# The first crossing of a two-block transformer kernel written in source order on three engines

## The chip, the cores and the metric

The kernel runs on one core of a Trainium2 chip. The metric is the device time of one execution in microseconds (us). The engines are named as the profile names them: PE (TensorE, matrix products), PEld (its weight loads), DVE (VectorE), ACT (ScalarE), POOL (GpSimd) and SP (SyncE, which issues the DMAs here). Matrix products and weight loads of PE overlap.

## What is computed

512 tokens of 1024 features pass a first block of two layers and then a second block of one layer. The part that the change touches is the start of a layer of the first block, and the mixers of the second.

```python
def first_block(x, g_pre_mix, w_in, ...):
    cos, sin = rope_tables(s)
    for l in range(DEPTH):                  # DEPTH = 2
        h = rms_norm(x, g_pre_mix[l])
        z = h @ w_in[l]
...
def rms_norm(x, g):
    xf = x.astype(jnp.float32)
    y = xf * lax.rsqrt(jnp.mean(xf * xf, axis=-1, keepdims=True) + RMS_EPS)
    return (y * g.astype(jnp.float32)).astype(x.dtype)
...
def second_block(x, c, rel_bias, ...):
        o_a = diff_attention(..., table_diff, lam_init)
        o_b = forgetting_attention(...)
        o_c = stick_breaking_attention(...)
        o_d = native_sparse_attention(..., table_nsa)
        mixed = jnp.concatenate([o_a, o_b, o_c, o_d], axis=-1) @ w_out[l]
```

Of `z`, the first columns are the queries, then keys and values of a band attention with 16 query heads, 4 key heads of 64 features and a rotary embedding (rope) on queries and keys. `table_diff` gives the differential attention a bias that depends on the distance of two tokens.

## The kernel before

Every fp32 product is made of three products of rounded halves: a tile `x` is split into `hi` (rounded, on ACT) and `lo = x − hi` (on DVE). `mm_kb` issues for one block of 128 features ("kb", 8 of them) hi by hi (L523), weight-hi by lo (L524) and weight-lo by hi (L525).

Weights come as units of 128 x 1024 numbers (512 KB), each holding 128 output columns for all 1024 features. `Stream` loads them in order into three raw buffers (L255, on SP), casts a unit to `wh` on ACT (L267) and subtracts to `wl` on DVE (L268); `cut_to(n)` says how far the casts are to be ahead of their use. A raw buffer is free for a further load once its unit is cast and subtracted.

The crossing (`cross`, L473 on) is the passage from one layer to the next, made in two halves of 256 tokens (`HV`). For one half, `chain1` loads x in four tiles of two feature blocks (`xh`), splits each (`scaled_split`: `hh` on ACT L447, `hl` on DVE L448) and adds its squares to `acc` (`add_sq`: squares on ACT L442, the first of them L437, sums on DVE L443). `Head.run` issues the products of the first three weight units with that half: two units of keys and one of queries, gathered in three PSUM tiles `hd`. `fin1` ends the rms norm of the half: eight one-column products of `acc` with ones (`pc`, L416), DVE L420, a power on POOL (L398), a diagonal `dg` on DVE (L427), one product with ones that spreads it (`pb`, L431), and a copy to `R` on ACT (L512). In layer 0 there is no layer ahead to end, and x comes straight from the input.

After the crossing, `layer` issues the values (`pv`, L559 to L561, 96 products of 256 columns), then the Q blocks one after the other (`ps`, 24 products of 512 columns each with one weight unit). `ropeR` (DVE L565) multiplies the rope tables with `R` of both halves; everything after it needs it: for each head `rope` does two steps on DVE (`t`, L573 and the shuffle L574) and two on POOL (L575, L576), and the result is cast and subtracted: KH on ACT (L587, L588) and KL on DVE (L589, L590) for keys, Q on ACT (L605) and DVE (L606) for queries, V on ACT (L596) and DVE (L597) for values. The number of casts ahead at this place is `CA = (3, 4)` for layers 0 and 1.

The order of the instructions of all engines is found by a scheduler that plays the program through a model of the chip, save where a part stands under `manual_schedule`: there the engines named take the order of the source. An engine executes its own list in order; semaphores make it wait for the others.

In the second block the mixers run as a pipeline of stages (`sb` for the stick-breaking heads, then `diff`, `fox` and `nsa`), each with a list of background pieces that prepare the next (`bg_sb` for the stage `sb`). `load_bias` reads the bias of four heads from a table in memory into four tiles F (L884).

Of the kernel before, what the change touches and what calls it, by code (L numbers as in the profile page):

```python
# [17 lines left out]
NB = 8  # L18
# [11 lines left out]
HV = ((0, 256), (256, 512))  # L30
# [249 lines left out]
class Kern:  # L280
# [181 lines left out]
    def cross(self, tail, chain, head, fin, early=0):  # L462
# [14 lines left out]
        if self.xdst[1][3] is not None:  # L477
            self.xsrc = self.xdst

    def chain1(self, i, pend, h, gname, acc2):  # L480
        nc = self.nc
        t0, t1 = HV[i]
        sl = slice(t0, t1)
        if pend:
            acc, mg, sqs = pend
            pb = self.bcast(self.rstd(acc, HV[i], sqs[i]), 2)
            Rp = self.half("Rp")
            nc.scalar.copy(Rp, pb[:, :256])

        def post():  # L490
            for j in range(4):
                xt = self.xload(i, j)
                if pend:
                    self.residual(xt, mg.t[j][:, :, sl], Rp, xt)
                for a in range(2):
                    kb = 2 * j + a
                    self.scaled_split(h.hi[kb][:, sl], h.lo[kb][:, sl], xt[:, a, :], self.col(gname, kb))
                self.add_sq(acc2[:, :, sl], xt, j == 0, nc.vector)
                if pend:
                    self.xstore(xt, i, j)  # L500

        return post
# [11 lines left out]
    def split(self, hi, lo, src):  # L514
        self.nc.scalar.copy(hi, src)
        self.nc.vector.tensor_sub(lo, src, hi.bitcast(F32))
# [23 lines left out]
    def layer(self, l, tail, pend):  # L540
        nc = self.nc
        h = Pair(self, "h", NB)
        acc2 = self.blk("acc2", [P, 2, T], F32)
        rs = {}
        head = Head(self, h, 3, seq=l == 0)
        self.cross(tail, lambda i: self.chain1(i, pend, h, f"g_pre_mix{l}", acc2), head,
                   lambda i: self.fin1(i, acc2, rs), early=1 if l == 0 else 0)
        rp = self.blk("rope", [P, 2, T], F32)
        nc.sync.dma_start(rp, self.a["rope"].rearrange("p (a t) -> p a t", a=2))
        pk = head.ps[0:2]  # L550
# [2 lines left out]
        for kb in range(NB):  # L553
            w = wv[kb // 4]
            sl = slice((kb % 4) * 256, (kb % 4) * 256 + 256)
# [44 lines left out]
        for m in range(NB):  # L600
            q = rope(head.ps[2] if m == 0 else self.mblock(h))
            for j in range(2):
                hd = 2 * m + j
# [580 lines left out]
    def block2(self, tail, pend):  # L1184
        nc = self.nc
        self.b2_consts()
        h = Pair(self, "h2", NB)
        head = Head(self, h, 4)
        acc2 = self.blk("acc2", [P, 2, T], F32)
# [35 lines left out]
        F = {}  # L1225
# [18 lines left out]
        def halves(x, ng):  # L1244
            v = x.rearrange("p t (a b) -> p t a b", a=ng)
            return [v[:, 0:2], v[:, 2:4]]

        def diff_prep():
            F["a"] = self.load_bias(0)
            box["zs"] = self.blk("zs", [P, 4 * 160], F32R)  # L1250
            box["ys"] = self.blk("ys", [P, 4 * 192], F32R)
            for a in range(2):
                t = self.blk("selraw", [P, 704], F32)
                nc.sync.dma_start(t, self.a["sel"][:, a * 704:(a + 1) * 704])
                for b in range(2):
                    nc.scalar.copy(box["zs"][:, (2 * a + b) * 160:(2 * a + b + 1) * 160], t[:, b * 352:b * 352 + 160])
                    nc.vector.tensor_copy(box["ys"][:, (2 * a + b) * 192:(2 * a + b + 1) * 192],
                                          t[:, b * 352 + 160:(b + 1) * 352])
# [63 lines left out]
        def osplit(m):  # L1322
# [4 lines left out]
        av = self.tm_group(h, 256, 4, self.v_pair(Va, 4), 2)  # L1327
# [6 lines left out]
        dfm = [P1(diff_fm, f) for f in range(4)]  # L1334
        sel = [[P1(diff_sel, f, p) for p in range(2)] for f in range(4)]
        bg_sb = [aq[0], aq[1], ak[0], aq[2], ak[1], diff_prep, dfm[0], ak[2], sel[0][0], av[0], dfm[2], sel[0][1],
                 sel[2][0], av[1], sel[2][1]]
        bg_diff = [g272[0], dfm[1], g272[1], sel[1][0], g272[2], dfm[3], g272[3], sel[1][1], sel[3][0], bq[0], ksw_norm,
                   sel[3][1], bq[1], fox_pre, bk[0], bq[2], bk[1], fox_pre2, bv[0], bk[2], P1(fox_q, 0), bv[1],
                   P1(fox_k, 0), P1(fox_k, 1)]  # L1340
# [45 lines left out]
        h = Pair(self, "h3", NB)  # L1386
        head = Head(self, h, self.NH3)
# [386 lines left out]
```

## Time and profile before

| | us |
|---|---|
| runs | 2470.20, 2470.53, 2471.22 |
| median | 2470.53 |
| the profiled execution | 2470.39 |
| its span | 2468.7 |
| PE busy in the span | 2404.3 (97%) |
| DVE busy | 1347.2 (55%) |
| ACT busy | 995.0 (40%) |
| POOL busy | 393.0 (16%) |

The span is the time from the first to the last instruction in the profile; 1.7 us of the profiled execution lie around it. PE stands for 90% of the chain that ended last. A share of busy time is a mean over stages, so what an edit of one stage can do is read from that stage's rows.

### The profile page before, as it was taken

How to read it: one execution, taken by the hardware profiler on the slowest of the kernel's cores; microseconds unless marked ns; L12 is line 12 of the kernel's file. 1: busy time of each engine (PE TensorE's matmuls, PEld its weight loads, DVE VectorE, ACT ScalarE, POOL GpSimd, SP SyncE). 2: the span in 40 equal slices, each digit the busy share in tenths (PEclk: the TensorE clock that was granted, in tenths of full speed). 3: DMA queues.
4: the chain of work that ended last, by engine and by line, in shares of the span. 5: the costliest groups of instructions: out<-in, count | busy, mean ns of one | idle time of the engine just before them, and what ended most of it. 6: DMA issues, size and time to landing. Idle time of an engine off the chain costs nothing.

```text
span 2468.7 us, 32508 instructions
## 1 busy us (share of the span) xinstructions
PE 2404.3 (97%) x12680; PEld 2069.8 (84%) x12680; DVE 1347.2 (55%) x2352; ACT 995.0 (40%) x1804; POOL 393.0 (16%) x437
## 2 busy tenths in 40 slices
PE   8999999999999999999999999999798899999999
PEld 7888888888888887888888888888788878888888
DVE  7777544366532188775443665321667686644531
ACT  4455423442223244554234422232375575333420
POOL 2423001211110033230012111100021133000000
PEclk9999999999999999999999999999899999999999
DMA  4211523355423232213233553232221204233250
GB/s 145 90 65 61 167 94 103 103 197 198 149 86 121 77 115 81 65 61 124 94 103 103 196 194 139 87 119 77 95 81 52 87 25 145 78 102 103 100 173 27
DMA packets 84995, 264.38 MB, mean 107 GB/s; under 512 B 9151, under 2 KB 17983, under 8 KB 84840
## 3 DMA queue, kind: packets, MB, share of 16 engines
q1 hardware_dynamic: 84840, 262.29, 31.5%
q8 instruction: 100, 1.64, 0.3%
q14 instruction: 55, 0.45, 0.1%
HBM read 249.65 MB, written 15.22 MB: 107 GB/s over the span
## 4 chain that ended last, share of the span: by engine, by line
PE 90%; DVE 5%; ACT 3%; issue 1%; POOL 1%; DMA 0%; SPq 0%; ACTq 0%; POOLq 0%; DVEq 0%
PE ps L523 24%; PE ps L525 24%; PE ps L524 24%; PE hd L524 2%; PE hd L525 2%; PE hd L523 2%; PE o L832 2%; PE pt L807 1%; PE tm L1017 1%; PE tm L1018 1%; PE tm L1019 1%; ACT pp L378 1%; PE s L783 1%; PE s L782 1%; PE s L1136 1%
## 5 line engine op out<-in xcount | busy, mean ns | idle before, releaser
L268 DVE TENSOR_TENSOR wl<-raw,wh 128x1024 fp32r<-128x1024 f32 x382 | 470.7, 1250 | 339.5 <-ACT wh L267 273.8
L267 ACT CAST wh<-raw 128x1024 fp32r<-128x1024 f32 x382 | 389.8, 1049 | 182.5 <-DMA raw<-in_w_dram 96.4
L525 PE MATMUL ps<-hh,wl 128*128 128x512 f32 x752 | 296.6, 394 | 5.5 <-DVE wl L268 5.5
L523 PE MATMUL ps<-hh,wh 128*128 128x512 f32 x752 | 295.6, 393 | 2.9 <-ACT wh L267 2.9
L524 PE MATMUL ps<-hl,wh 128*128 128x512 f32 x752 | 295.3, 393 | 0.0
L524 PE MATMUL ps<-hfl,wh 128*128 128x512 f32 x640 | 249.3, 390 | 0.0
L523 PE MATMUL ps<-hfh,wh 128*128 128x512 f32 x640 | 249.1, 390 | 0.0
L525 PE MATMUL ps<-hfh,wl 128*128 128x512 f32 x640 | 248.9, 389 | 0.0
L525 PEld LDWEIGHTS ps<-hh,wl 128*128 128x128 f32 x752 | 141.7, 188 | 33.8 <-DVE wl L268 6.8
L523 PEld LDWEIGHTS ps<-hh,wh 128*128 128x128 f32 x752 | 141.8, 189 | 30.5 <-ACT wh L267 3.4
L524 PEld LDWEIGHTS ps<-hl,wh 128*128 128x128 f32 x752 | 141.8, 189 | 27.6
L525 PE MATMUL ps<-hidh,wl 128*128 128x512 f32 (+1 forms) x396 | 145.1, 366 | 0.0
L523 PE MATMUL ps<-hidh,wh 128*128 128x512 f32 (+1 forms) x396 | 144.9, 366 | 0.0
L524 PE MATMUL ps<-hidl,wh 128*128 128x512 f32 (+1 forms) x396 | 144.7, 365 | 0.0
L525 PEld LDWEIGHTS ps<-hfh,wl 128*128 128x128 f32 x640 | 120.1, 188 | 25.0
L524 PEld LDWEIGHTS ps<-hfl,wh 128*128 128x128 f32 x640 | 120.2, 188 | 24.6
L523 PEld LDWEIGHTS ps<-hfh,wh 128*128 128x128 f32 x640 | 120.0, 188 | 24.8
L378 ACT ACTIVATE pp<-pp,at_nm 128x256 f32<-128x256 f32 (+1 forms) x208 | 114.4, 553 | 62.6 <-DVE at_nm L789 54.3
L712 POOL TENSOR_TENSOR gs<-gs,R 128x512 f32<-128x512 f32 x44 | 70.0, 1590 | 379.1 <-ACT gs L378 368.1
L524 PE MATMUL ps<-h3l,wh 128*128 128x512 f32 x320 | 124.5, 389 | 0.0
L525 PE MATMUL ps<-h3h,wl 128*128 128x512 f32 x320 | 124.5, 389 | 0.0
L523 PE MATMUL ps<-h3h,wh 128*128 128x512 f32 x320 | 124.3, 389 | 0.0
(462 smaller groups left out, 5208.6 us busy)
## 6 DMA issues: line engine op xcount, KB each, us to landing
raw<-in_w_dram SPq DMA_DIRECT2D x382, 512.0 KB, 3.6
adaraw<-in_ada_dram SPq DMA_DIRECT2D x48, 512.0 KB, 5.7
xd<-xh SPq DMA_DIRECT2D x24, 256.0 KB, 2.1
xh<-xd SPq DMA_DIRECT2D x24, 256.0 KB, 3.4
xh<-in_x_dram SPq DMA_DIRECT2D x16, 256.0 KB, 5.1
bias_d<-row_d SPq DMA_DIRECT2D x8, 320.0 KB, 6.1
xd<-fg SPq DMA_DIRECT2D x8, 256.0 KB, 3.2
F<-bias_d SPq DMA_DIRECT2D x8, 256.0 KB, 5.5
```

What stands on the lines that cost most here:

```text
L267: nc.scalar.copy(hi, raw)
L268: nc.vector.tensor_sub(lo, raw, hi.bitcast(F32))
L378: i = nc.scalar.activation(out, in_, func, **kw)
L523: nc.tensor.matmul(ps[:, t], w[0][:, sl], h.hi[kb][:, t], start=first, stop=False)
L524: nc.tensor.matmul(ps[:, t], w[0][:, sl], h.lo[kb][:, t], start=False, stop=False)
L525: nc.tensor.matmul(ps[:, t], w[1][:, sl], h.hi[kb][:, t], start=False, stop=last)
L712: nc.gpsimd.tensor_mul(g, g, self.R)
L782: nc.tensor.matmul(ps[:, :n], q, KH[g][:, LO[i]:HI[i]], start=True, stop=False)
L783: nc.tensor.matmul(ps[:, :n], q, KL[g][:, LO[i]:HI[i]], start=False, stop=True)
L807: nc.tensor.transpose(bank[:, c0:c0 + P], pslice(h, i)[:, c:c + P], self.ident)
L832: nc.tensor.matmul(ps[:, c0:c1], V[j][:, g * P:(g + 1) * P], t[b][:, a, c0:c1], start=(a == 0 and j == 0), stop=(a == 1 and j == 2))
L1017: nc.tensor.matmul(o, h.hi[kb][:, tsl], w[0][:, sl], start=kb == 0 and i == 0, stop=False)
```

## The change

The crossing of layer 0 gets a function of its own, `cross0`, whose instructions on PE, DVE and ACT stand under `manual_schedule` and so run in source order. Weight unit 1 is cast ahead of the later tiles of x; the squares of a tile come behind splits; PE takes the first four feature blocks of two weight units, then the last four, then the third unit; the second half goes tile by tile; both `fin` calls stand at the end. Layer 1 keeps `cross`. In the second block the loads of the bias for the differential attention leave the piece `diff_prep` and become a piece of their own, later in the list `bg_sb`; the scheduler orders the stage anew from that.

```diff
--- before.py
+++ after.py
@@ -477,6 +477,56 @@
         if self.xdst[1][3] is not None:
             self.xsrc = self.xdst
 
+    def cross0(self, h, head, gname, acc2, fin):
+        E = mybir.EngineType
+        xt = {}
+
+        def split(i, j):
+            sl = slice(*HV[i])
+            xt[j] = self.xload(i, j)
+            for a in range(2):
+                kb = 2 * j + a
+                self.scaled_split(h.hi[kb][:, sl], h.lo[kb][:, sl], xt[j][:, a, :], self.col(gname, kb))
+
+        def square(i, j):
+            self.add_sq(acc2[:, :, slice(*HV[i])], xt.pop(j), j == 0, self.nc.vector)
+
+        def unit():
+            head.w.append(self.st.next(ahead=0))
+            head.ps.append(self.ps("hd"))
+
+        def mm(i, j, kbs):
+            for kb in kbs:
+                self.mm_kb(head.ps[j], head.w[j], h, kb, kb == 0, kb == NB - 1, hv=HV[i])
+
+        with self.tc.manual_schedule(engines={E.PE, E.DVE, E.Activation}):
+            unit()
+            split(0, 0)
+            split(0, 1)
+            mm(0, 0, range(4))
+            unit()
+            mm(0, 1, range(4))
+            square(0, 0)
+            split(0, 2)
+            square(0, 1)
+            split(0, 3)
+            mm(0, 0, range(4, 8))
+            mm(0, 1, range(4, 8))
+            unit()
+            square(0, 2)
+            square(0, 3)
+            mm(0, 2, range(8))
+            for j in range(4):
+                split(1, j)
+                square(1, j)
+                for kb in (2 * j, 2 * j + 1):
+                    for n in range(3):
+                        mm(1, n, [kb])
+                if j in (1, 2):
+                    self.st.cut_to(self.st.used + j)
+            fin(0)
+            fin(1)
+
     def chain1(self, i, pend, h, gname, acc2):
         nc = self.nc
         t0, t1 = HV[i]
@@ -542,9 +592,12 @@
         h = Pair(self, "h", NB)
         acc2 = self.blk("acc2", [P, 2, T], F32)
         rs = {}
-        head = Head(self, h, 3, seq=l == 0)
-        self.cross(tail, lambda i: self.chain1(i, pend, h, f"g_pre_mix{l}", acc2), head,
-                   lambda i: self.fin1(i, acc2, rs), early=1 if l == 0 else 0)
+        head = Head(self, h, 3)
+        fin = lambda i: self.fin1(i, acc2, rs)
+        if l:
+            self.cross(tail, lambda i: self.chain1(i, pend, h, f"g_pre_mix{l}", acc2), head, fin)
+        else:
+            self.cross0(h, head, f"g_pre_mix{l}", acc2, fin)
         rp = self.blk("rope", [P, 2, T], F32)
         nc.sync.dma_start(rp, self.a["rope"].rearrange("p (a t) -> p a t", a=2))
         pk = head.ps[0:2]
@@ -1245,8 +1298,10 @@
             v = x.rearrange("p t (a b) -> p t a b", a=ng)
             return [v[:, 0:2], v[:, 2:4]]
 
+        def diff_bias():
+            F["a"] = self.load_bias(0)
+
         def diff_prep():
-            F["a"] = self.load_bias(0)
             box["zs"] = self.blk("zs", [P, 4 * 160], F32R)
             box["ys"] = self.blk("ys", [P, 4 * 192], F32R)
             for a in range(2):
@@ -1334,7 +1389,7 @@
         dfm = [P1(diff_fm, f) for f in range(4)]
         sel = [[P1(diff_sel, f, p) for p in range(2)] for f in range(4)]
         bg_sb = [aq[0], aq[1], ak[0], aq[2], ak[1], diff_prep, dfm[0], ak[2], sel[0][0], av[0], dfm[2], sel[0][1],
-                 sel[2][0], av[1], sel[2][1]]
+                 sel[2][0], av[1], diff_bias, sel[2][1]]
         bg_diff = [g272[0], dfm[1], g272[1], sel[1][0], g272[2], dfm[3], g272[3], sel[1][1], sel[3][0], bq[0], ksw_norm,
                    sel[3][1], bq[1], fox_pre, bk[0], bq[2], bk[1], fox_pre2, bv[0], bk[2], P1(fox_q, 0), bv[1],
                    P1(fox_k, 0), P1(fox_k, 1)]
```

PE at the start of the first half: `hd_168` and `hd_124` are the first unit's tiles, `hd_155` is the second unit's, `pc_277` belongs to the norm. Before:

```order
L523 MATMUL hd_168<-hh_12_129,wh_8_116 128x256
L524 MATMUL hd_168<-hl_13_130,wh_8_116 128x256
L525 MATMUL hd_168<-hh_12_129,wl_9_117 128x256
L523 MATMUL hd_168<-hh_15_138,wh_8_116 128x256
L416 MATMUL pc_277<-ones,acc_7_115 128x1 x4
L524 MATMUL hd_168<-hl_16_139,wh_8_116 128x256
L525 MATMUL hd_168<-hh_15_138,wl_9_117 128x256
L523 MATMUL hd_168<-hh_15_138,wh_8_116 128x256
L524 MATMUL hd_168<-hl_16_139,wh_8_116 128x256
```

and after, the same places of PE's list:

```order
L573 MATMUL hd_124<-hh_13_131,wh_8_118 128x256
L574 MATMUL hd_124<-hl_14_132,wh_8_118 128x256
L575 MATMUL hd_124<-hh_13_131,wl_9_119 128x256
L573 MATMUL hd_155<-hh_11_125,wh_15_149 128x256
L574 MATMUL hd_155<-hl_12_126,wh_15_149 128x256
L575 MATMUL hd_155<-hh_11_125,wl_16_150 128x256
L573 MATMUL hd_155<-hh_11_125,wh_15_149 128x256
L574 MATMUL hd_155<-hl_12_126,wh_15_149 128x256
L575 MATMUL hd_155<-hh_11_125,wl_16_150 128x256
```

The `pc` group has left this place, and after twelve products the second weight unit (`wh_15`) is needed.

PE at the second `pb` (`pb_302` before, `pb_388` after); `pv` are the values' tiles, `ps` the first Q block. Before:

```order
L525 MATMUL hd_170<-hh_18_147,wl_24_163 128x256
L559 MATMUL pv_403<-wh_45_305,hh_10_122 128x256
L560 MATMUL pv_403<-wl_46_306,hh_10_122 128x256
L561 MATMUL pv_403<-wh_45_305,hl_11_123 128x256
L559 MATMUL pv_403<-wh_45_305,hh_10_122 128x256
L560 MATMUL pv_403<-wl_46_306,hh_10_122 128x256
L561 MATMUL pv_403<-wh_45_305,hl_11_123 128x256
L559 MATMUL pv_404<-wh_45_305,hh_10_122 128x256
L560 MATMUL pv_404<-wl_46_306,hh_10_122 128x256
L561 MATMUL pv_404<-wh_45_305,hl_11_123 128x256
L431 MATMUL pb_302<-dg_300,ones 128x256
L559 MATMUL pv_404<-wh_45_305,hh_10_122 128x256
```

and after:

```order
L612 MATMUL pv_406<-wh_35_330,hh_21_178 128x256
L431 MATMUL pb_388<-dg_386,ones 128x256
L613 MATMUL pv_406<-wl_36_331,hh_21_178 128x256
L614 MATMUL pv_406<-wh_35_330,hl_22_179 128x256
L612 MATMUL pv_407<-wh_35_330,hh_21_178 128x256
L613 MATMUL pv_407<-wl_36_331,hh_21_178 128x256
L614 MATMUL pv_407<-wh_35_330,hl_22_179 128x256
L612 MATMUL pv_407<-wh_35_330,hh_21_178 128x256
L613 MATMUL pv_407<-wl_36_331,hh_21_178 128x256
L614 MATMUL pv_407<-wh_35_330,hl_22_179 128x256
L573 MATMUL ps_567<-hh_11_125,wh_50_394 128x512
L574 MATMUL ps_567<-hl_12_126,wh_50_394 128x512
```

The second `pb` stood behind nine `pv` products; now eight `pv` products are left behind it before the first Q block.

ACT at the copies to `R`, with the weight casts ahead of them. Before:

```order
L267 CAST wh_47_311<-raw_160 128x1024
L267 CAST wh_49_317<-raw_166 128x1024
L512 COPY R<-pb_288 128x256
L267 CAST wh_52_397<-raw_309 128x1024
L267 CAST wh_56_501<-raw_315 128x1024
L512 COPY R<-pb_302 128x256
L587 CAST KH_62_517<-t_60_511 64x512
```

and after:

```order
L267 CAST wh_50_394<-raw_212 128x1024
L267 CAST wh_52_400<-raw_301 128x1024
L267 CAST wh_56_504<-raw_334 128x1024
L562 COPY R<-pb_374 128x256
L562 COPY R<-pb_388 128x256
L640 CAST KH_62_520<-t_60_514 64x512
```

The two copies to `R` (L512 before, L562 after) stood apart, with two casts between them; now they follow each other behind the casts of three units.

## Rows read from the trace of the kernel before

**Rows 1.** Windows: us, busy us of each engine (x instructions), PEclk, DMA share, GB/s
```profile
6.66:12.82 6.16, 5.36 (x22) 4.73 (x22) 6.05 (x15) 6.16 (x13) 0.00 (x0) 1.00 1.04 389
...
17.19:60.00 42.81, 42.81 (x293) 39.92 (x292) 30.54 (x52) 17.47 (x30) 14.21 (x11) 1.00 0.26 88
60.00:70.00 10.00, 7.95 (x34) 5.95 (x33) 9.24 (x11) 4.57 (x6) 6.32 (x4) 1.00 0.21 61
```

**Rows 2.** Timeline of PE, first crossing: start, us, line, operation, [idle before <-releaser]
```profile
10.54 0.41 PE L523 MATMUL hd<-hh,wh 128*128 128x256 f32 x1
11.09 1.86 PE L416 MATMUL pc<-ones,acc 128*128 128x1 f32 x8
...
27.48 0.95 PE L416 MATMUL pc<-ones,acc 128*128 128x1 f32 x8
```

**Rows 3.** Timeline of SP, ACT and DVE, the first weights
```profile
3.73 0.94 SPq L255 DMA_DIRECT2D raw<-in_w_dram  x2
...
5.16 1.04 ACT L267 CAST wh<-raw 128x1024 fp32r<-128x1024 f32 x1 [3.07 <-DMA raw<-in_w_dram]
...
6.23 1.23 DVE L268 TENSOR_TENSOR wl<-raw,wh 128x1024 fp32r<-128x1024 f32 x1 [4.93 <-ACT wh L267]
```

**Rows 4.** Tile view of raw, 3.6 to 12.5 us
```profile
DMA to landing us min/median/max: 6.3/6.7/7.1
```

**Rows 5.** Timeline of PE, second half of layer 0's values
```profile
32.92 0.59 PE L431 MATMUL pb<-dg,ones 128*128 128x256 f32 x2
...
43.78 0.40 PE L523 MATMUL ps<-hh,wh 128*128 128x512 f32 x1
```

**Rows 6.** Timelines of ACT, DVE and PE, layer 0
```profile
33.55 0.37 ACT L512 COPY R<-pb 128x256 f32<-128x256 f32 x1 [4.78 <-PE pb L431]
...
33.96 1.23 DVE L565 TENSOR_TENSOR ropeR<-rope,R 128x1024 f32<-128x1024 f32 x1 [3.59 <-ACT R L512]
...
49.36 0.88 DVE L597 SCALAR_TENSOR_TENSOR V<-pv,rs_r,V 128x256 fp32r<-128x256 f32 x2
...
57.96 1.05 ACT L267 CAST wh<-raw 128x1024 fp32r<-128x1024 f32 x1
...
60.14 2.19 DVE L268 TENSOR_TENSOR wl<-raw,wh 128x1024 fp32r<-128x1024 f32 x1
...
62.38 0.50 PE L525 MATMUL ps<-hh,wl 128*128 128x512 f32 x1 [1.64 <-DVE wl L268]
```

**Rows 7.** Timeline of DVE, the same place of layer 1
```profile
900.27 1.23 DVE L565 TENSOR_TENSOR ropeR<-rope,R 128x1024 f32<-128x1024 f32 x1 [3.32 <-ACT R L512]
...
917.38 0.88 DVE L597 SCALAR_TENSOR_TENSOR V<-pv,rs_r,V 128x256 fp32r<-128x256 f32 x2
...
918.88 1.41 DVE L606 TENSOR_TENSOR Q<-t,Q 64x512 fp32r<-64x512 f32 x2
...
921.89 2.73 DVE L606 TENSOR_TENSOR Q<-t,Q 64x512 fp32r<-64x512 f32 x2
924.64 0.69 DVE L573 TENSOR_TENSOR t<-ps,ropeR 128x512 f32<-128x512 f32 x1
...
926.02 2.37 DVE L606 TENSOR_TENSOR Q<-t,Q 64x512 fp32r<-64x512 f32 x2
928.41 2.18 DVE L268 TENSOR_TENSOR wl<-raw,wh 128x1024 fp32r<-128x1024 f32 x1
```

**Rows 8.** Windows of layer 1, PE alone: us, busy us, PEclk, DMA share, GB/s
```profile
923.50:930.60 7.10, 0.78 (x3) 0.86 0.00 0
930.60:935.40 4.80, 4.75 (x11) 0.50 0.35 111
```

**Rows 9.** Tile view of F, 1790 to 1900 us
```profile
L1137 DVE CUSTOM_DVE_ANT_0 pp<-s,F x16: 284/484/686, 1853.3 to 1888.5; 128x384 f32<-128x384 f32 x4, 128x128 f32<-128x128 f32 x4, 128x256 f32<-128x256 f32 x4, 128x512 f32<-128x512 f32 x4
...
DMA to landing us min/median/max: 3.7/5.9/6.0
```

**Rows 10.** Waits of PE: us in total, times, longest
```profile
PE o L1174 <- ACT sbt L515: 2.6, 3, 1.3
```

## Prediction

> **What bounds the kernel now.** I read the windows view first. TensorE (PE) is the bound almost everywhere: from 17.19 to 60.00 us it is busy for all 42.81 us, and in the first stage, 6.66 to 12.82, for 5.36 of 6.16 [rows 1]. In the ten microseconds after 60 it is idle for 10.00 − 7.95 = 2.05 us [rows 1]. An edit of the first crossing can therefore win only three things: idle time ahead of 17 us, time at the lower clock there, and the 2.05 us. It can lose wherever PE is fed just in time.
>
> The PE timeline of the start comes next [rows 2]. The group of eight short `pc` matmuls takes 1.86 us at 11.09 and 0.95 us at 27.48: the first microseconds run at the lower of the two clock levels (1.2 GHz), although the granted-clock column prints 1.00 there. In before, PE gets through 13 `hd` matmuls (the thirteenth starts at 10.54), takes the `pc` group, and goes on at 12.82, the end of the first window of rows 1.
>
> The third view is the chain that PE waits for after 60 us, followed backwards over three engines [rows 6]. PE waits until 62.38 for `wl` of the fourth Q block (DVE, 60.14, 2.19 us). This needs `wh` (ACT, 57.96), which stands behind the K, V and Q casts of the first heads. Those need `ropeR` (DVE, 33.96), which waits for the copy of R of the second half (ACT, 33.55), and that for the second `pb` on PE at 32.92 [rows 5]. So the place of the second `pb` in PE's order sets when the fourth Q block gets its weights, and the slack is already used up: before waits there.
>
> **The change part by part: the start.** The new order does four contraction blocks of `hd0`, 12 matmuls, and then needs unit 1, whose cast now stands ahead of the later splits. What limits that cast is its transfer: issued at 3.73 [rows 3], landing after at least 6.3 us [rows 4], so at about 10.1. Cast 1.04 and subtract 1.23 [rows 3] put `wl` at 12.4, and PE goes on at 12.45 with 14 `hd` matmuls done (two need `wh` alone) where before went on at 12.82 with 13. That is 0.37 plus one matmul of 0.21 ahead. But before took its `pc` group inside that wait; after takes it later, for about 0.8 us (0.95 less the overlap of its end [rows 2]). Net +0.25 us. The bounds are −1.9 (the higher level comes at 12.5 instead of 17.2: 4.7 us of work would shrink by 0.12/0.21, 2.1 less, and with the +0.25 about −1.9) and +0.5. I take +0.25. The squares moved behind the splits I cost at nothing: the next splits of DVE run beside the ten matmuls of `hd1` that are left at 12.45 (2.1 us at 0.21); if that cover is too thin, it is in the +0.5.
>
> **The second `pb`.** Both `fin` calls now stand at the end of the crossing. In PE's order the second `pb` has eight `pv` matmuls left between it and the first `ps` of the Q blocks, which ran at 43.78 [rows 5]; before it had 87. By rows 5: 43.78 + 0.25 − 8 × 0.12 − 0.24 = 42.8. R follows 0.63 later (32.92 to 33.55), `ropeR` 0.41 after that [rows 5, 6]: 43.9 instead of 33.96, **9.9 us later**. The chain `pc`, `rs_v`, power, `dg` between them is covered by some 30 `pv` matmuls of 0.12, about 3.8 us; it costs nothing on PE.
>
> **From `ropeR` to the fourth Q block.** The 72 matmuls of three Q blocks, plus the eight `pv`, keep PE busy until about 60.4 (43.78 + 72 × 0.227 + 0.25). What DVE has to do from `ropeR` to `wl` stands in layer 1 of before, where `pb` is late already and the order on DVE is nearly the one that layer 0 now gets [rows 7]:
> - `ropeR` 900.27 to the first V at 917.38: 17.1 us, with the same list of operations.
> - V, one `t`, a pair of Q, a shuffle, V: 917.38 to 921.89, 4.5 us.
> - then half a Q pair, `t`, shuffle, the other half: a pair takes 1.33 (918.88, 1.41 with overlap), and `t` with shuffle 1.38 (924.64 to 926.02): 2.7 us.
> - `wl` 2.18.
>
> 43.9 + 17.1 + 4.5 + 2.7 = 68.2, and `wl` ends at 70.4; PE goes on at 70.45 instead of 62.38 [rows 6], +8.07. The second wait of before, 2.05 − 1.64 = 0.41 [rows 1, 6], disappears behind it. **+7.7 us.** The +0.25 of the start is inside this sum, not beside it. Bounds: layer 0 of before needed 15.4 us to V (49.36 [rows 6]) plus 0.7 for one `t` more, and a `wl` with nobody beside it takes 1.23 [rows 3], which together gives 2.0 less: +5.7. By layer 1's whole list up to the end of `wl` (930.59) it is 30.3 us, and PE would go on at 74.2: +11.5. I take +7.7, the operations that this order really has.
>
> Here DVE rows swell when POOL works: a pair of Q takes 1.41 at 918.88 and 2.73 at 921.89 [rows 7]. The Trainium skill ("SBUF — State Buffer", section "SBUF: two separate sides") says why such a thing happens: the port pair of VectorE and GpSimd is a lock, held for a whole instruction, not shared bandwidth. By that rule the Q halves ahead of `wl` could swell too, 1.3 more; the rows would then give +9.0 in place of +7.7.
>
> **The clock.** Layer 1 shows what such a pair of pauses does: from 923.50 to 930.60 PE is busy for 0.78 of 7.10 us, and the next 4.80 us are granted 0.50, the lower level: 11 matmuls take 4.75 us [rows 8]. At 0.227 a matmul (62.38 less the pause of 1.64, to 43.78, is 74 of them) these take 2.5, so the drop costs **+2.2 us**. In after PE would have two matmuls in 60.4 to 70.45, a longer pause than that, so I count one such drop; before's pause of 1.64 at 62.38 had none. Bounds: 0 and 3.2. The Trainium skill ("TensorE: Matmul & The Clock Gate", section "What's actually happening") has it that "the default state is throttled, and activity releases the throttle", which speaks against any edit that opens a pause; if it did not hold here the sum would be 2.2 less.
>
> **The bias loads of block 2.** The four F loads leave `diff_prep` and go behind `av[1]`. Nothing is added. But on SP they now stand behind two further weight loads, each of which waits for a raw buffer, and their memory is one that the stage before frees only with its last contractions. First use is at 1853.3, and a load lands after 3.7 to 6.0 us [rows 9]. What that leaves cannot be read from rows. It is between −2.6 (the scheduler's new order of this stage takes away all three waits for `sbt` [rows 10]) and +6.0 (a full landing is exposed). I take 0: the stage still hides the landing, as it hides all loads of before but those few waits.
>
> **Sum.** 2470.39 (profiled execution, 0.14 under the median 2470.53) + 7.7 + 2.2 + 0 = 2480.3. Against the median this is +9.8, or 0.4%.
>
> **Rivals.**
> - A, no drop of the clock: the two matmuls between the pauses suffice. 2470.4 + 7.7 = 2478.1. Against it: rows 8. Chance 0.15.
> - B, the bias comes late: F reaches `pp` a landing of 3.7 after the scores are there [rows 9], on top of the forecast: 2484.0, or 2486.2 if that pause too lowers the clock. For it: two loads ahead on SP and memory that comes free late. Against it: 3 us or so of other matmuls in that stage. Chance 0.17.
> - C, the chain is short: +5.7, no drop, and the start's −1.9 moves `pb` and everything behind it forward: 2470.4 + 5.7 − 1.9 = 2474.2, within 0.2%. For it: layer 0 had fewer swollen rows than layer 1 (15.4 to V). Against it: it needs three favourable ends together. Chance 0.12.
> - D, faster: block 2 carries it. If the bias moved away frees the stage of all the `sbt` waits (2.6) and, with C's chain and an early clock, the fourth Q block finds its weights, the time is 2470.4 − 2.6 − 2.05 − 0.4 = 2465.3. It decides at one point: `ropeR` at 35.8 or sooner (43.9 − 8.1). With 79 more matmuls of 0.12 ahead of `pb` in PE's order that cannot be. Chance 0.02.
> - E, the cast of unit 1 isn't sooner, since its transfer ends at 10.1 whatever the order says. This is part of the forecast already: the intended gain is 0.5 us at most.
>
> **How the numbers follow.** Forecast 0.54, A 0.15, B 0.17, C 0.12, D 0.02. A measurement of this kernel tells apart about 0.2%, 4.9 us. Faster by over that: D, 0.02. Within: C, and 0.02 of the forecast with the lower chain and the `sbt` waits gone, 0.14. Slower: 0.84. The range leaves out C's lower half, D and the upper third of B: 2474.3 to 2486.5; its upper part also holds the chain by layer 1's whole list (+11.5 + 2.2 = 2484.1).
>
> **What would show it.** Right: PE goes on at about 12.4 after 14 `hd` matmuls; second `pb` at 42.8, `ropeR` at 43.9; PE idle from 60.4 with two matmuls until about 70.4; granted clock 0.50 behind it; an unchanged sum from 1790 to 1890. Wrong: `wh` of unit 1 before 10; a second `pb` ahead of 40; a `wl` at 66 or sooner; a pause of PE at the first scores with F. The forecast falls if the wait ahead of the fourth Q block stays under 5 us.

## The result, and the profile after

| | before | after |
|---|---|---|
| runs beside each other | 2470.20 to 2472.39 (five) | 2479.28, 2480.57, 2484.11, 2487.37, 2488.74 |
| median | 2471.03 | 2484.11 |
| ratio, with 95% interval | | 1.0052 [1.0036, 1.0068] |
| the profiled execution | 2470.39 | 2488.74 |
| PE busy | 2404.3 | 2413.1 |

The change makes the kernel slower by 13.1 us in the medians, 0.5%. The forecast was 2480.3 with a range of 2474.3 to 2486.5. A later set of seven runs of the same kernel, beside 20 other runs of before (median 2472.60), had a median of 2479.65 and a ratio of 1.0033 [1.0017, 1.0048]. All twelve runs of the changed kernel together have a median of 2480.1. The profile shown here is of the slowest of the first five.

Timeline of PE of the kernel after, at the start, then at the norm ends and the fourth Q block (start, us, line, operation, in brackets the idle time before it and what ended it); these rows answer to [rows 2, 5] and the last of [rows 6]:

```profile
10.57 0.41 PE L575 MATMUL hd<-hh,wl 128*128 128x256 f32 x1
11.72 0.58 PE L573 MATMUL hd<-hh,wh 128*128 128x256 f32 x1 [0.73 <-ACT wh L267]
...
12.98 0.58 PE L575 MATMUL hd<-hh,wl 128*128 128x256 f32 x1 [0.47 <-DVE wl L268]
...
30.96 0.95 PE L416 MATMUL pc<-ones,acc 128*128 128x1 f32 x8
...
35.69 0.59 PE L431 MATMUL pb<-dg,ones 128*128 128x256 f32 x2
...
38.99 0.95 PE L416 MATMUL pc<-ones,acc 128*128 128x1 f32 x8
...
43.72 0.60 PE L431 MATMUL pb<-dg,ones 128*128 128x256 f32 x2
...
66.06 0.79 PE L573 MATMUL ps<-hh,wh 128*128 128x512 f32 x1 [4.46 <-ACT wh L267]
...
71.70 0.79 PE L575 MATMUL ps<-hh,wl 128*128 128x512 f32 x1 [4.41 <-DVE wl L268]
```

Timeline of DVE of the kernel after, from `ropeR` to the `wl` that PE waits for; in layer 0 now what [rows 7] show of layer 1:

```profile
44.75 1.23 DVE L618 TENSOR_TENSOR ropeR<-rope,R 128x1024 f32<-128x1024 f32 x1 [3.38 <-ACT R L562]
...
62.42 0.87 DVE L650 SCALAR_TENSOR_TENSOR V<-pv,rs_r,V 128x256 fp32r<-128x256 f32 x2
...
69.46 2.18 DVE L268 TENSOR_TENSOR wl<-raw,wh 128x1024 fp32r<-128x1024 f32 x1
```

The second `pb` runs at 43.72 and not at 32.92, `ropeR` at 44.75 and not at 33.96, and PE goes on with the fourth Q block at 71.70 and not at 62.38. The two pauses ahead of it last 4.46 and 4.41 us where before had 1.64.

Windows of the kernel after (us, busy us of each engine with instructions, PEclk, DMA share, GB/s), which answer to [rows 1] and [rows 8]:

```profile
18.25:61.50 43.25, 43.25 (x296) 40.08 (x294) 26.92 (x45) 16.13 (x27) 13.84 (x11) 1.00 0.25 86
61.50:71.70 10.20, 1.33 (x4) 0.51 (x3) 9.92 (x17) 5.31 (x8) 7.04 (x5) 0.72 0.00 0
71.70:76.50 4.80, 4.80 (x12) 3.78 (x13) 4.67 (x5) 2.29 (x3) 1.07 (x1) 0.53 0.40 123
```

In the ten microseconds of the pauses PE is busy for 1.33, and DVE for 9.92 of 10.20: PE waits for DVE, which is busy nearly all the time. Behind them the granted clock is 0.53 over 4.8 us: nearly all of it is at the lower level, 1.2 GHz.

To see where the rest lies, the same matmul was looked for in both traces, and its start in before subtracted from its start in the other kernel:

| start later than in before, us | at the crossing to layer 0's FFN (494.6 in before) | 40 us on | in layer 1's Q blocks | in layer 1's FFN | end |
|---|---|---|---|---|---|
| after | 10.7 | 13.4 | 14.5 | 16.8 | 17.2 |
| cross_only | 8.5 | 8.6 | 9.8 | 8.9 | 8.2 |
| bias_only | 0.6 | 0.6 | 0.6 | 2.9 | 3.5 |
| late_pb_end | 7.7 | 7.7 | 7.7 | 7.6 | 7.5 |
| combo4 | −1.6 | −0.2 | 1.0 | 0.3 | 0.1 |

For the kernel after, the first column is the loss of the first crossing with its two pauses. The source between that column and block 2 is unchanged, yet this execution loses 6 us more there. Most of it is clock. Both traces have the same pause at the crossing to the FFN, 1.7 us of idle PE time in six or seven. Windows of before, then of after (columns as above):

```profile
493.00:496.00 3.00, 1.65 (x11) 1.27 (x10) 3.00 (x7) 2.73 (x7) 0.06 (x1) 1.00 0.39 145
496.00:499.00 3.00, 2.69 (x22) 2.70 (x23) 3.00 (x8) 3.00 (x8) 0.82 (x1) 1.00 0.91 308
499.00:503.00 4.00, 4.00 (x34) 3.95 (x33) 4.00 (x7) 3.51 (x6) 0.00 (x0) 1.00 0.53 165
```

```profile
503.00:505.00 2.00, 1.65 (x14) 1.48 (x13) 2.00 (x4) 0.99 (x3) 0.00 (x0) 1.00 0.01 4
505.00:507.00 2.00, 0.73 (x4) 0.53 (x4) 2.00 (x6) 2.00 (x6) 0.32 (x1) 0.83 0.71 258
507.00:510.00 3.00, 2.95 (x14) 2.95 (x15) 3.00 (x7) 3.00 (x7) 0.56 (x1) 0.50 0.81 273
510.00:514.00 4.00, 4.00 (x22) 3.95 (x22) 3.04 (x6) 1.08 (x2) 0.00 (x0) 0.61 0.62 182
```

Before keeps the higher level behind its pause; after is granted 0.50 behind the same one, and some 28 products of 256 columns take 0.213 instead of 0.120 us: 2.6 us, the step from 10.7 to 13.4 in the table. At the second such crossing (1375) it is the same again: granted 0.52 from 1373 to 1380 in after, 1.00 from 1359 to 1366 in before. The scatter of the runs is of this size and comes in steps: seven later runs of after lie at 2478 to 2480 (five of them), 2486.6 and 2491.7. Each run's mean granted clock goes with it: 0.990 in the seven runs of after at 2478 to 2481, 0.986 to 0.988 in the five at 2484 to 2492.

Two executions of the one kernel can be laid beside each other too, after and after_again. Their matmuls keep within 0.2 us of each other up to 1985. Then the same wait of 0.82 us comes in both; behind it after is granted 1.00 (1999.7 to 2003.1), after_again 0.55 (2002 to 2005), and the matmul behind the wait takes 0.50 and 0.80 us. After_again had waited 0.6 us more for a load about 13 us earlier. Timelines of PE, after, then after_again:

```profile
1999.34 0.50 PE L1227 MATMUL o<-ptb,Va 128*128 128x512 f32 x1 [0.82 <-ACT ptb L565]
...
2001.37 0.80 PE L1227 MATMUL o<-ptb,Va 128*128 128x512 f32 x1 [0.82 <-ACT ptb L565]
```

The step of some 1.2 us ahead of layer 1's Q blocks is neither clock nor scatter. With the new crossing of layer 0 the scheduler also orders layer 1's crossing anew: DVE does the four `fg` ahead of a `wl`, and PE waits 1.19 us for it. Before does that `wl` first and has no such wait. After_again, cross_only, pb_early, combo2, combo3 and combo4 have the wait too. PE and DVE of after, then DVE of before:

```profile
891.64 0.39 PE L575 MATMUL hd<-hh,wl 128*128 128x256 f32 x1 [1.19 <-DVE wl L268]
...
887.96 2.49 DVE L556 TENSOR_TENSOR fg<-fg,Rp 128x512 f32<-128x512 f32 x4
890.37 1.22 DVE L268 TENSOR_TENSOR wl<-raw,wh 128x1024 fp32r<-128x1024 f32 x1
...
874.60 1.22 DVE L268 TENSOR_TENSOR wl<-raw,wh 128x1024 fp32r<-128x1024 f32 x1
875.73 2.49 DVE L506 TENSOR_TENSOR fg<-fg,Rp 128x512 f32<-128x512 f32 x4
```

### The profile page after: what moved, and what is told of

Read it like the earlier page. It is cut to its first block, busy times and chain, and to the rows that moved or that the text cites. A ratio compares the mean times of both kernels' runs of the same rounds, so it can differ in the third digit from the quotient of the medians.

```text
span 2485.9 us, 32505 instructions
## 1 busy us (share of the span) xinstructions
PE 2413.1 (97%) x12680; PEld 2078.3 (84%) x12680; DVE 1345.4 (54%) x2352; ACT 994.9 (40%) x1804; POOL 389.6 (16%) x437
## 4 chain that ended last, share of the span: by engine, by line
PE 91%; DVE 5%; ACT 2%; issue 1%; DMA 1%; POOL 0%; SPq 0%; ACTq 0%; DVEq 0%; POOLq 0%
PE ps L573 24%; PE ps L575 24%; PE ps L574 24%; PE hd L574 2%; PE hd L575 2%; PE hd L573 2%; PE o L885 2%; PE pt L860 1%; PE tm L1070 1%; PE tm L1071 1%; PE tm L1072 1%; PE s L836 1%; PE s L835 1%; ACT pp L378 1%; PE s L1189 1%
```

## The experiments

My theory (P in the expectations): the loss comes from the place of the second `pb`, through `ropeR` and DVE's work to the fourth Q block. Its rivals: the bias loads carry part of it (B), the new source order costs by itself (S), and, for versions with a better start, that the gain is lost ahead of the same Q block (W).

**cross_only**, the change without its part in block 2.

```diff
-        def diff_bias():
+        def diff_prep():
             F["a"] = self.load_bias(0)
-
-        def diff_prep():
...
-                 sel[2][0], av[1], diff_bias, sel[2][1]]
+                 sel[2][0], av[1], sel[2][1]]
```

> The change without its part in block 2: the bias loads stay in diff_prep. Theory P (the place of the second pb): the whole loss comes from the first crossing, so the time is that of the changed kernel, 2479 to 2489, ropeR at about 44.7, PE waiting twice for 4.4 us at 61.6 to 71.7. Rival B (the bias loads in block 2 cost part of it): 4 us or more is gone, 2475 to 2480, with the crossing's rows unchanged.

Measured: 2481.32, ratio 1.0041 [1.0026, 1.0055]. PE waits 4.45 and 4.41 us and goes on at 70.02, `ropeR` runs at 43.09. This execution has no lower clock at the crossing to the FFN, and its loss at that point, 8.5 us, is still its loss at the end, 8.2. So the first crossing is enough for the loss. The median lies in P's range, 1.3 us above B's; the scatter doesn't allow to tell 2 us apart, and the next run does. That 8.5 is less than the 10.7 of after is no matter of the bias: the three engines' lists at the start are those of after, but the higher clock came at 15.4 us and not at 18.2, and 1.7 us of the difference stand there by 20 us already.

**bias_only**, the kernel before with the bias loads moved.

```diff
+        def diff_bias():
+            F["a"] = self.load_bias(0)
+
         def diff_prep():
-            F["a"] = self.load_bias(0)
...
-                 sel[2][0], av[1], sel[2][1]]
+                 sel[2][0], av[1], diff_bias, sel[2][1]]
```

> The kernel before with only the bias loads moved behind av[1]. Theory P: within 2 us of before, 2469 to 2473; waits in block 2 change places but not their sum. Rival B: 2475 or more, with PE or DVE waiting at the first scores that use F.

Measured: 2469.98, ratio 0.9995 [0.9986, 1.0003]: no difference that can be seen. What block 2's new order does to the waits stands in the waits of PE (us in total, times, longest), of bias_only:

```profile
PE tm L1017 <- DVE ksw L1232: 4.1, 1, 4.1
...
PE sel L1282 <- DVE Va L1027: 3.2, 2, 2.6
...
PE o L1174 <- ACT sbt L515: 0.7, 1, 0.7
```

Before had 3.8 for `ksw`, nothing for `Va` and 2.6 for `sbt` [rows 10]: waits change places. F itself is waited for by nobody. In the kernel after its four loads are issued from 1866.35 on, only 6 us ahead of the first use, and land 2.5 us after their issue (the tile view of F, 1790 to 1910):

```profile
L1190 DVE CUSTOM_DVE_ANT_0 pp<-s,F x16: 282/480/692, 1872.6 to 1906.4; 128x384 f32<-128x384 f32 x4, 128x128 f32<-128x128 f32 x4, 128x256 f32<-128x256 f32 x4, 128x512 f32<-128x512 f32 x4
L937 SPq DMA_DIRECT2D F<-bias_d x4: 326/428/431, 1866.4 to 1867.7; - x4
...
DMA to landing us min/median/max: 2.5/2.5/2.5
```

**late_pb_mid and late_pb_end**, the kernel before with nothing but a later `fin1` of the second half.

```diff
 # cross, layer 0
         fin(0)
-        fin(1)
+        if tail:
+            fin(1)
 # layer, behind the values' products of feature block kb
+            if kb == 1 and not l:           # late_pb_end: kb == 3
+                self.fin1(1, acc2, rs)
```

> The kernel before with one move: fin1 of the second half of layer 0 is issued after the values' products of two feature blocks, so that its pb has 41 pv products left behind it instead of 87. Start, splits, squares, casts and bias as before. Theory P (the pb's place alone sets the wait): pb at 38.6, ropeR at 39.7, PE goes on with the fourth Q block at about 66.4, 4 us later than before, time 2473 to 2477 with the clock's scatter of about 2. Rival S (the source order of the crossing costs, not the pb): 2470 to 2473, as before.

> As late_pb_mid, but after four feature blocks: 17 pv products are left behind the pb, in the changed kernel eight. Theory P: pb at 41.5, ropeR at 42.6, PE goes on at about 69.3 (before 62.4), with a stretch at the lower clock behind it; 2477 to 2482. Rival S: 2470 to 2473.

Measured: late_pb_mid 2478.67, 1.0031 [1.0019, 1.0043]; late_pb_end 2477.95, 1.0026 [1.0015, 1.0037]. Timelines of DVE and PE of late_pb_end, then its windows:

```profile
43.10 1.23 DVE L568 TENSOR_TENSOR ropeR<-rope,R 128x1024 f32<-128x1024 f32 x1 [3.38 <-ACT R L513]
...
63.85 0.50 PE L524 MATMUL ps<-hh,wh 128*128 128x512 f32 x1 [2.94 <-ACT wh L267]
69.30 0.80 PE L526 MATMUL ps<-hh,wl 128*128 128x512 f32 x1 [4.72 <-DVE wl L268]
```

```profile
60.90:69.30 8.40, 0.74 (x3) 0.30 (x2) 8.21 (x14) 5.12 (x8) 3.28 (x3) 0.78 0.00 1
69.30:72.40 3.10, 3.10 (x7) 2.51 (x8) 3.00 (x4) 0.00 (x0) 2.28 (x2) 0.50 0.48 167
```

With the old start, the old splits and casts and the old bias, the late `pb` alone brings back the two pauses, the lower clock and 7.2 us. Rival S falls as the cause of this loss: it had 2470 to 2473. The half step doesn't come out by its time, which is no lower than that of the full step. Its trace shows `ropeR` at 37.42, not at 39.7. The higher clock came at 11.4 us there and at 17.2 in before, although the lists of PE, ACT and DVE are the same up to 27 us; what follows runs 2.2 us earlier by that, and with these 2.2 us added `ropeR` stands where it was expected. PE goes on at 64.22, and at the crossing to the FFN late_pb_mid is 3.6 us behind before (some 5.7 without the early clock, by adding the 2.2 again), late_pb_end 7.7. What late_pb_mid loses behind that point (7.8 at the end) goes with stretches of lower clock that before has not, at the crossing to the FFN (granted 0.57 from 499 to 503) and in block 2.

**pb_early and combo**, both norm ends early, by source order. The first half's norm goes into the second half's products, the second half's `pc` ahead of the last two feature blocks, its `pb` behind twelve `pv`. Combo has another start besides (squares, not shown, come behind all splits of the half), and the bias as before. Left-out lines are marked with three dots.

```diff
+                if j == 3:
+                    pre(1)                  # pc, rs_v, power
                 for kb in (2 * j, 2 * j + 1):
                     for n in range(3):
                         mm(1, n, [kb])
+                if j == 0:
+                    pre(0)
+                if j == 1:
+                    post(0)                 # dg, pb, copy to R on ACT
...
-            fin(0)
-            fin(1)
+            return self.values(h, lambda: post(1))
 # combo: the start
             mm(0, 0, range(4))
-            unit()
-            mm(0, 1, range(4))
...
             split(0, 2)
...
             split(0, 3)
             mm(0, 0, range(4, 8))
...
+            unit()
+            mm(0, 1, range(8))
```

> The changed kernel with the two fin calls taken apart and moved: the first half's norm stands inside the second half's products, the second half's pc ahead of the products of kb 6 and 7, its pb behind twelve pv products; the values' products are in the same source order. All else as changed, the bias too. Theory P: the second pb is back at 33 to 34.5, ropeR at 34 to 35.5, the waits ahead of the fourth Q block fall from 8.9 to 1.5 to 4 us without a drop of the clock there, and the time is 2470 to 2474. Rival S (the new source order of splits, casts and squares costs by itself): 2477 or more although ropeR is early.

> As pb_early, with the bias loads in diff_prep again and with another start: all four tiles of the first half are split ahead of the cast of unit 1, and PE does all eight blocks of hd0 first. Theory P with the transfer of unit 1 as the limit of the start: PE has no pause between 8.3 and 30, 24 hd products by about 12.9, the second pb at 31.5 to 33, time 2466 to 2470. Rival W (the wait for the first weights only moves to unit 1 or 2): a pause of over 1 us at 12 to 15, 2470 or more.

Measured: pb_early 2485.30, 1.0048 [1.0033, 1.0063]; combo 2479.24, 1.0036 [1.0021, 1.005]. Both expectations of P fail, since the `pb` did not come early. Timelines of PE and ACT of pb_early:

```profile
27.09 0.60 PE L431 MATMUL pb<-dg,ones 128*128 128x256 f32 x2
29.50 0.39 PE L599 MATMUL hd<-hh,wh 128*128 128x256 f32 x1 [1.81 <-ACT hh L447]
30.75 0.58 PE L600 MATMUL hd<-hl,wh 128*128 128x256 f32 x1 [0.86 <-DVE hl L448]
...
41.62 0.59 PE L431 MATMUL pb<-dg,ones 128*128 128x256 f32 x2
...
27.73 0.37 ACT L628 COPY R<-pb 128x256 f32<-128x256 f32 x1 [9.18 <-PE pb L431]
...
42.52 2.95 ACT L267 CAST wh<-raw 128x1024 fp32r<-128x1024 f32 x3
```

In source order ACT stood 9.18 us at the copy of R of the first half; the next splits were queued behind it, PE waited for them, fell to the lower clock (granted 0.50 from 30.2 to 40.2) and reached the second `pb` at 41.62. The three casts behind the second copy brought three subtracts on DVE ahead of `ropeR` (43.60 to 47.10), which ran at 47.02. The runs don't test S, but they do test the second half of P: PE goes on at 73.86, 26.8 us after `ropeR`. Combo's start did what was expected: no pause of PE between 7.84 and the `pc` at 21.01.

**pb_early2 and combo2**, the same without that wait: the first copy of R behind all splits, splits one tile ahead.

```diff
+                if j < 3:
+                    split(1, j + 1)
+                    square(1, j + 1)
...
+                if j == 1:
+                    pb0 = self.bcast(fin[1][0], 2)
...
+                if j == 2:
+                    R(0, pb0)
+                    fin[0](1)               # pc and rs_v of the second half
+                    self.st.cut_to(self.st.used + 3)
```

> As pb_early (the changed kernel with both norm ends early), but without what stopped it: the copy of R of the first half, for which ACT made the later splits wait, stands behind all splits, the splits are one tile ahead, and the casts of units 5 to 7 stand ahead of the second R. Seven products of Q blocks come in among the crossing's. Theory P: ropeR at 33 to 36, no pause of PE over 1.5 us before 60, PE goes on with the fourth Q block at 61 to 64, 2469 to 2473. Rival S: 2477 or more with ropeR as early as that.

> As pb_early2, with all four splits of the first half ahead of the cast of unit 1 (combo's start, which had no pause of PE from 7.8 to 21) and the bias loads in diff_prep. Theory P: ropeR at 32 to 34, the fourth Q block at 59 to 62, 2466 to 2470. Rival W (the start's gain is lost again in front of the fourth Q block): the wait there grows by what the start gains, 2470 to 2473.

Measured: pb_early2 2478.32, 1.0023 [1.0011, 1.0035]; combo2 2474.18, 1.0011 [1.0003, 1.002]. `ropeR` runs at 37.90 and 36.08 (expected 33 to 36 and 32 to 34; it waits about 2 us for the rope tables, whose load now stands behind weight loads), PE goes on at 64.53 and 62.77 after two pauses each, the second of 1.63 and 1.64. At the crossing to the FFN pb_early2 is 3.4 us behind before and the kernel after 10.7: of the loss there, two thirds are gone with the order of splits, casts and squares of the change kept. Its time did not follow in full: behind that point 5.3 us come on top (8.7 at the end), most of it at crossings with the lower clock. By its time pb_early2 lies in S's range and not in P's. So S isn't needed for the loss (late_pb_end), but that the new order of splits, casts and squares costs nothing by itself is not shown.

**combo3 and combo4**. combo3 loads the rope tables sooner, puts the `pc` of the first half inside its own third unit and the second `pb` right behind the crossing's last product; combo4 also casts units 6 and 7 ahead of the second copy of R.

```diff
 # combo3 (beside combo2)
+            mm(0, 2, range(4))
+            fin[0](0)                       # pc, rs_v, power of the first half
...
+                if j == 2:
+                    rope()                  # load of the tables
 # combo4 (beside combo3)
+            pb1 = self.spread(dg)
+            self.st.cut_to(self.st.used + 5)
-            R(1, self.spread(dg))
+            R(1, pb1)
```

> As combo2, with what still held ropeR up taken away: the load of the rope tables stands ahead of the weight loads that the later casts free, the first half's pc stands inside its own third unit, so that DVE no longer waits for it ahead of a split, and the second pb stands right behind the crossing's last product. Theory P: ropeR at 31 to 33, no wait of PE at the fourth Q block, 2465 to 2469. Rival W (the wait for wl there is DVE's own work and not the pb any more): PE still waits over 1 us at 59 to 62, 2469 to 2473.

> As combo3, with one thing moved: the casts of units 6 and 7 stand ahead of the second copy of R on ACT, not behind it, so that their subtracts no longer stand between R and ropeR on DVE. Theory P: ropeR at 31.3 instead of 34.4, wl of the fourth Q block ends at about 58 where PE needs it at 58.6, the wait of 2.5 is gone, and the 2 us that the start gains stay: 2466 to 2471. Rival W (DVE's work between R and that wl is the bound whatever comes ahead): a wait of over 1.5 us stays, 2470 to 2475 as combo3.

Measured: combo3 2473.16, 1.0005 [0.9996, 1.0015]; combo4 2470.59 beside 2472.60, 0.9993 [0.9983, 1.0003]. Timelines of DVE and PE of combo4:

```profile
27.84 3.49 DVE L268 TENSOR_TENSOR wl<-raw,wh 128x1024 fp32r<-128x1024 f32 x3
31.25 2.06 DVE L662 TENSOR_TENSOR ropeR<-rope,R 128x1024 f32<-128x1024 f32 x1
...
58.22 1.23 DVE L268 TENSOR_TENSOR wl<-raw,wh 128x1024 fp32r<-128x1024 f32 x1
...
59.50 0.50 PE L625 MATMUL ps<-hh,wl 128*128 128x512 f32 x1 [1.38 <-DVE wl L268]
```

In combo3 `ropeR` stood at 34.41 behind two subtracts, and the wait was 2.51, over the 1 us that W names. But combo3 does not lose its start there: it was 2.1 us ahead of before, before waits 1.64 and 0.41 at this place itself, and behind it combo3 is still 1.9 us ahead. In combo4 `ropeR` comes at 31.25 as P expected, but a wait of 1.38 stays, which P had at zero: with DVE that early, it waits 0.38 us for a Q block of PE at 52.27 and 1.76 for ACT's cast of Q at 55.38. Behind the fourth Q block combo4 is 3.6 us ahead of before.

What combo3 and combo4 have won is lost further on. PE of combo3, from the fourth Q block on, then DVE and POOL of combo3, then DVE and POOL of before at the same place:

```profile
61.12 0.50 PE L623 MATMUL ps<-hh,wl 128*128 128x512 f32 x1 [2.51 <-DVE wl L268]
85.27 0.50 PE L623 MATMUL ps<-hh,wl 128*128 128x512 f32 x1 [0.23 <-DVE wl L268]
92.11 0.50 PE L623 MATMUL ps<-hh,wl 128*128 128x512 f32 x1 [1.10 <-DVE wl L268]
...
89.85 2.21 DVE L268 TENSOR_TENSOR wl<-raw,wh 128x1024 fp32r<-128x1024 f32 x1
...
89.18 1.80 POOL L670 TENSOR_TENSOR t<-t,ropeR 128x512 f32<-128x512 f32 x1 [2.82 <-DVE t L669]
...
89.86 1.21 DVE L268 TENSOR_TENSOR wl<-raw,wh 128x1024 fp32r<-128x1024 f32 x1
...
90.05 2.17 POOL L575 TENSOR_TENSOR t<-t,ropeR 128x512 f32<-128x512 f32 x1 [3.52 <-DVE t L574]
```

In before the subtract for `wl` starts ahead of POOL's step and takes 1.21 us; in combo3 half a Q pair stands ahead of it on DVE, POOL's step has started, and it takes 2.21. PE waits for it, and before has no wait between 78 and 100 us. Pb_early2, combo2, combo3 and combo4 all have these two waits and lose 1.9 us between 80 and 97. So combo3 is level with before at the crossing to the FFN, and combo4 keeps 1.6 us (table above). No run takes these waits away. In the whole time the 1.6 us of combo4 are not told apart from before, and no version beats the kernel before beyond the scatter.

How much of what the combos win at the start comes from its order isn't shown either. Their higher clock comes at 10.4 to 13.3 us, in before at 17.2; but late_pb_mid, with the start of before, was 2.2 us ahead at the same place too.

**after_again**, the kernel after unchanged.

> The changed kernel once more, beside the same runs of before as combo4. Theory P: 2479 to 2489 again, ropeR at 43.9 to 44.8, two pauses of about 4.4 us at 61 to 72. Whether the lower clock comes at the crossings at 505 and 1375 may differ from the first profile: if it does, the time differs by about 2.5 us for each.

Measured: 2479.65, with the profile of the slowest run: `ropeR` 44.66, pauses of 4.49 and 4.41, lower clock at 507 and 1374 again, 20.6 us later at the end.

What ties the runs together is the time from the start of `ropeR` to the matmul that had waited for `wl`:

| | `ropeR` | PE goes on | between |
|---|---|---|---|
| combo4 | 31.25 | 59.50 | 28.25 |
| before | 33.96 | 62.38 | 28.42 |
| combo3 | 34.41 | 61.12 | 26.71 |
| bias_only | 34.52 | 62.94 | 28.42 |
| combo2 | 36.08 | 62.77 | 26.69 |
| late_pb_mid | 37.42 | 64.22 | 26.80 |
| pb_early2 | 37.90 | 64.53 | 26.63 |
| cross_only | 43.09 | 70.02 | 26.93 |
| late_pb_end | 43.10 | 69.30 | 26.20 |
| combo | 43.41 | 70.28 | 26.87 |
| after_again | 44.66 | 71.64 | 26.98 |
| after | 44.75 | 71.70 | 26.95 |
| pb_early | 47.02 | 73.86 | 26.84 |

Over 16 us of `ropeR`, with different starts, orders and bias places, it is 26.2 to 28.4. PE's own products before that point are the same 334 in all. So the place of `ropeR`, set against PE's own progress, sets the wait.

## Why the prediction was right, and where it fell short

**The direction and the mechanism** came out, and the time lay in the range. The start: PE on at 12.98 after 14 `hd` products (12.45 expected; its first product was 0.37 later because the first weights landed later in this execution). The second `pb`: 43.72 (42.8). `ropeR`: 44.75 (43.9). From `ropeR` to PE: 26.95 (26.55 by the list of layer 1's operations). PE on at 71.70 (70.45). Two matmuls between the pauses, which begin at 61.6 (60.4), and the lower clock behind them: ten products at 0.427 (eleven counted), 2.0 us (2.2). PE has no wait between 12.98 and 61.5, so the squares behind the splits cost nothing, as assumed. The loss by the crossing to the FFN is 10.7; the sum had 7.7 + 2.2 = 9.9. Of the 0.8 between them 0.4 is the later landing, and an estimate of 0.45 the higher clock, which came at 18.2 us and not at 17.2 (1.02 us at 0.213 in place of 0.120 a product). That it agrees so closely is in part luck: the same lists at the start gave 8.5 in cross_only. The reading of the layer ahead as a pattern for the layer that gets its order held to half a microsecond.

**Why the `pb` is late** is more than its place in the source, as the prediction had it. PE's order must keep the first half's `pb` ahead of the second half's `pc`, so two norm chains stand one after the other: `pc` 30.96, `pb` 35.69, `pc` 38.99, `pb` 43.72, with values' products between. The second `dg` was ready at 41.4. Of the 4.7 us from `pc` to `pb` each chain needs some 2.4; the rest is the place of `pb` behind `pv` products.

**The step that failed** is the last term of the sum: block 2 at 0 was right (bias_only), but with it I had set everything behind layer 0 at 0, and counted the clock once. The profile after has lower clock at two crossings more, 2.7 us at 505 and about 2.4 at 1375, and the wait of 1.19 us at layer 1's crossing that the scheduler's new order makes. The scatter that goes with the clock (2479 to 2489) puts the median of the first five runs 4 us over the forecast; the median of all twelve, 2480.1, lies on it. The forecast knew nothing of this scatter, so that it meets that median so closely is luck in part. My sentence that the pause of 1.64 in before had no drop behind it held at this place in every run with pauses of 1.4 to 2.5 there (bias_only, combo2, combo3, combo4, pb_early2); at the crossing to the FFN 1.7 us of idle time in seven, and later a wait of 0.82, were followed by the lower level in one trace and not in the other.

**The rivals.** A (no drop in layer 0) fell: 0.53 behind the pauses. B (bias late) has its mechanism half, since F is issued 6 us ahead of its use, and costs nothing (bias_only): the loads land in 2.5 us and not in 3.7 to 6.0. C and D fell with `ropeR`. E held: unit 1's cast waits for its transfer (`wh` at 10.63 on ACT, after 1.78 us of idle ended by the DMA).

The Trainium skill's sentence that "the default state is throttled, and activity releases the throttle" ("TensorE: Matmul & The Clock Gate", section "What's actually happening") agrees with the rows of 61.50 to 76.50. The windows of 503 to 514 beside those of 493 to 503 show what this sentence leaves open: behind two like pauses the clock fell once and once not.

## What to carry to other kernels

A stage that another engine must finish (here the norm's end on PE, before DVE's rope) is scheduled by its consumer, not by where its inputs are ready: ask how long the consumer's work is up to the next wait of the bounding engine, and set the producer that far ahead. Source order on an in-order engine makes every short copy a gate for all that is queued behind it; before fixing an order by hand, look for copies and small products that wait for another engine, and put them where that engine has long been done. Expect a gain at one place to be lost again where another engine feeds the bounding one just in time: here 1.9 us were, at subtracts that POOL's steps had got ahead of. And before a gain is credited to an order, compare when the higher clock came.

## What the runs showed of the hardware

- The same pause can be followed by the lower clock in one execution and not in another (0.82 us at 1999 in after and at 2001 in after_again). At the crossing to layer 0's FFN such a stretch cost 1.3 us (late_pb_mid) to 2.7 us (after). Before itself, in 20 runs beside combo4, lies between 2467.62 and 2479.05.
- The four loads of F land 2.5 us after issue when nothing else is in flight (after, DMA share 0.00 from 1864.0 to 1866.3) and after 3.7 to 6.0 beside weight loads [rows 9].
- A subtract for `wl` takes 1.21 us when it starts ahead of POOL's step and 2.21 when that step has started (89.86 in before, 89.85 in combo3); POOL's step takes 2.17 in the first case and 1.80 in the second.
- At the start the lower level ends at 10.4 (combo4), 17.2 (before) or 18.2 us (after). Combo4 has no pause of PE there after 7.75, but late_pb_mid, with the same lists at the start as before, reached the higher level at 11.4 too, and cross_only, with the lists of after, at 15.4: one order gives times some 6 us apart. So the order alone doesn't explain it. What does is open.
